# First feed-forward layer of a decoder block: the seven-product down stage with tokens standing, its sums turned once by VectorE

## The chip, the cores and the metric

The kernel runs on one core of a Trainium2 chip. The metric is the device time of one execution in microseconds (us), as the median of several. All matmuls work on float32 data that is split into a high and a low part.

## The reference

One decoder layer with 512 tokens (T) and 1024 channels (D): a half-step SwiGLU feed-forward layer, a token mixer, and a second half-step feed-forward layer, each with a norm before and one after. The change concerns only the first of them:

```
def swiglu(x, w_gu, w_down):
    gate, up = jnp.split(x @ w_gu, 2, axis=-1)
    return (jax.nn.silu(gate) * up) @ w_down

x = x + 0.5 * rms_norm(swiglu(rms_norm(x, ffn1_pre_g), ffn1_w_gu, ffn1_w_down), ffn1_post_g)
```

The hidden width is 2816, that is 22 chunks of 128.

## The kernel before

**Stages.** The hidden chunks of the first layer go in five groups: 0 to 3, 4 to 7, 8 to 11, 12 to 15 and 16 to 21. Group 0 is done plainly. For the others the gate and up products (`octo`) are made with seven products of blocks instead of eight, tokens standing in the array; the hidden values of four chunks are turned by VectorE's transposes (tile `za`), written to HBM (`h_a`) by four transfers on SyncE's queue, and read back (`hxa`) into the seven forms that the down stage needs (`seven_forms_of`). `Hidden.high` and `Hidden.low` make the high and the low part of each form.

**The down stage of a group** (`seven_down`) also takes seven products in place of eight, named a11, s3, a12, s2, s4, a22 and s1, for a block of weights of two chunks by 512 channels each. It is called for the groups that start at chunks 4, 8 and 12. The function `one` that it is given makes one product in two PSUM banks. Before, that is `by_channels`: 128 by 128 weights stand, 256 tokens move, three matmuls for each pair of a high and a low part, 24 matmuls a product. ScalarE copies the banks into a `stage` tile, and GpSimd adds the tile into HBM by a transfer with `accum_op=ALU.add`. The sums `yp_a` in HBM are laid out by channels, as the later steps want them: partitions are channels, columns are tokens. Group 0 writes them first.

**The last group** computes its down product plainly for eight chunks of 128 channels, c = 0 to 7. Before it, SyncE reads the sums back from HBM as `parts` (tiles `yp_a` in SBUF). The loop over c takes chunks 0 to 4 at once: six hidden chunks by three matmuls of 512 tokens into a bank `ya`, then VectorE adds the part (`Residual.chunk`, line 676 in the profile), ScalarE squares it, and GpSimd adds the square to `acca_r` (line 686). Chunks 5, 6 and 7 are late: `boundary` makes them in halves of 256 tokens (`ay`), first all three first halves, then the second halves. VectorE adds parts (L692) and squares (L705, L709), and in the middle of chunk 6's second half TensorE makes the sums of squares (`rms_r`, L550). While chunks are computed, ScalarE rounds later weights to their high part and VectorE subtracts to get the low part (`wlo_ad` for the down weights, `wlo_xl` for the mixer's, line 215).

In the same loop stand small tasks for the mixer that comes next: `load_gates`, `masks` (GpSimd fills and selects the attention mask in the tile `home`, VectorE copies it to `up`), `split_gates`, and `give_back`, by which GpSimd reads the residual's x back (`xT`).

**What sets the order.** Each engine executes its instructions in the order in which the program issues them, and so do the queues of transfers. `W` is the planner of weights: raw weights have five buffers (`tag="raw"`); when a raw buffer's last low part is made, it loads the next weights, or, where `W.owed` has an entry, calls that in its place. For the last group `W.owed` holds two entries that do nothing, so two loads are left out there:

```
            if f1 == FC:
                W.owed = [lambda: None] * 2
```

## Time and profile before

| | |
|---|---|
| time, median of 3 runs | 843.34 us (843.26 to 843.58) |
| the profiled execution's own time | 842.55 us |
| its span, from first to last instruction | 840.8 us |
| TensorE (PE) busy | 832.2 us, 99% |
| VectorE (DVE) busy | 723.8 us, 86% |
| ScalarE (ACT) busy | 520.9 us, 62% |
| GpSimd (POOL) busy | 162.6 us, 19% |
| the three down stages by channels, about | 155 to 175, 213 to 233, 271 to 292 us |
| the last group's down product and its late halves, about | 310 to 344 us |

In rows of the timeline the first two numbers are the start and the time taken, then come the engine, the line of the program, the operation, what it writes and reads, its shape and how many instructions the row holds; the brackets tell how long the engine was idle before it and what ended that. `SPq` and `POOLq` rows are issues of transfers. In rows of the windows, the columns are the window, its length, the busy time of each engine asked for (with its instructions), the granted TensorE clock, the share of the transfer engines and GB/s.

### The profile page before, as it was taken

Reading aid. Unit: us, or ns where it says so; the run is one execution under the profiler, and the core shown is the slowest. Engines: PE = TensorE matmul, PEld = TensorE weight load, DVE = VectorE, ACT = ScalarE, POOL = GpSimd, SP = SyncE. Lnnn points to the kernel's source line nnn. Section 1 sums busy time; section 2 is a strip of 40 time slices with the busy share of each in tenths; the row PEclk is TensorE's granted clock in tenths of the full one; section 3 lists DMA queues with packets and bytes.
Section 4 is the critical chain, followed back from the end, with each engine's and each line's share of the span. In section 5 each row is a group of like instructions: output and inputs, shape, how many; then the busy total and the mean of one; then the engine's idle time right before and its main releaser. Section 6 shows DMA issues by size and latency. Waiting matters only on the chain.

```text
span 840.8 us, 12378 instructions
## 1 busy us (share of the span) xinstructions
PE 832.2 (99%) x4504; PEld 718.9 (85%) x4504; DVE 723.8 (86%) x1026; ACT 520.9 (62%) x821; POOL 162.6 (19%) x178
## 2 busy tenths in 40 slices
PE   9999999999999999999999999999999999999996
PEld 8988888988988998987788899888888888888885
DVE  4978999998989965879889589799999899898996
ACT  6646756666666655556797456536758667666562
POOL 2023000140320333304531052002004114032001
PEclk9999999999999999999999999999999999999999
DMA  7249429398595799323511131169439939769842
GB/s 252 77 128 347 135 79 318 80 251 267 123 255 186 167 261 331 93 62 108 157 51 51 51 105 47 50 129 290 179 106 232 317 92 257 253 149 258 305 140 101
DMA packets 123614, 143.73 MB, mean 171 GB/s; under 512 B 23897, under 2 KB 81569, under 8 KB 123041
## 3 DMA queue, kind: packets, MB, share of 16 engines
q1 hardware_dynamic: 109232, 111.86, 42.0%
q0 software_dynamic: 14176, 30.94, 17.0%
q8 instruction: 35, 0.57, 0.3%
q14 instruction: 27, 0.21, 0.1%
q10 hardware_dynamic: 144, 0.13, 0.0%
HBM read 100.45 MB, written 40.89 MB: 168 GB/s over the span
## 4 chain that ended last, share of the span: by engine, by line
PE 96%; DVE 2%; DMA 1%; SPq 0%; issue 0%; ACT 0%; DVEq 0%; ACTq 0%
PE aa L951 10%; PE ab L951 10%; PE db L951 5%; PE da L951 5%; PE yaa L1347 3%; PE bb L951 3%; PE ba L951 3%; PE yda L1347 2%; PE ya L506 2%; PE ya L507 2%; PE ya L508 2%; PE aa L881 1%; PE a_first L1206 1%; PE yab L1884 1%; PE yab L1885 1%; PE yab L1886 1%
## 5 line engine op out<-in xcount | busy, mean ns | idle before, releaser
L1116 POOL DMA_DIRECT2D yp_a<-stage x42 | 36.8, 1064 | 182.6 <-ACT stage L1113 158.8
L1116 POOL DMA_DIRECT2D yp_b<-stage x42 | 36.4, 1084 | 144.3 <-ACT stage L1113 117.8
L506 PE MATMUL ya<-hha,whi_ad 128*128 128x512 f32 x62 | 24.1, 389 | 0.0
L507 PE MATMUL ya<-hla,whi_ad 128*128 128x512 f32 x62 | 24.1, 389 | 0.0
L508 PE MATMUL ya<-hha,wlo_ad 128*128 128x512 f32 x62 | 24.1, 389 | 0.0
L686 POOL TENSOR_TENSOR acca_r<-acca_r,sq_r 128x512 f32<-128x512 f32 x6 | 8.1, 1357 | 61.7 <-ACT sq_r L536 61.7
L1900 POOL DMA_DIRECT2D yp_b<-stage x8 | 4.3, 548 | 67.1 <-ACT stage L1899 67.1
L524 PE MATMUL an<-xh_mx,whi_xl 128*128 128x256 f32 x64 | 15.9, 289 | 0.0
L525 PE MATMUL an<-xh_mx,wlo_xl 128*128 128x256 f32 x64 | 15.5, 283 | 0.0
L2003 POOL TENSOR_TENSOR last<-yp,grow 128x512 f32<-128x512 f32 x3 | 3.9, 1290 | 57.2 <-DVE yp L1993 57.2
L2000 ACT ACTIVATE ysq<-yp 128x512 f32<-128x512 f32 (+1 forms) x8 | 4.8, 606 | 16.2 <-DVE yp L1993 16.2
L506 PE MATMUL gt<-xh_mx,whi_gt 128*128 128x512 f32 x32 | 14.3, 445 | 0.0
L508 PEld LDWEIGHTS ya<-hha,wlo_ad 128*128 128x128 f32 x62 | 11.6, 188 | 2.4
L506 PEld LDWEIGHTS ya<-hha,whi_ad 128*128 128x128 f32 x62 | 11.6, 188 | 2.4
L507 PEld LDWEIGHTS ya<-hla,whi_ad 128*128 128x128 f32 x62 | 11.6, 188 | 2.4
L536 ACT ACTIVATE sq_r<-yp_a 128x256 f32<-128x256 f32 (+1 forms) x10 | 5.0, 502 | 12.9 <-DVE yp_a L676 5.9
L506 PE MATMUL pq<-xh_mx,whi_q 128*128 128x512 f32 x32 | 12.8, 399 | 0.0
L506 PE MATMUL pub<-xh_f,whi_bu 128*128 128x512 f32 x32 | 12.6, 395 | 0.0
L508 PE MATMUL gt<-xh_mx,wlo_gt 128*128 128x512 f32 x32 | 12.6, 394 | 0.0
L506 PE MATMUL pgb<-xh_f,whi_bg 128*128 128x512 f32 x32 | 12.6, 393 | 0.0
L507 PE MATMUL gt<-xl_mx,whi_gt 128*128 128x512 f32 x32 | 12.6, 392 | 0.0
L508 PE MATMUL pgb<-xh_f,wlo_bg 128*128 128x512 f32 x32 | 12.5, 390 | 0.0
(2014 smaller groups left out, 3468.8 us busy)
## 6 DMA issues: line engine op xcount, KB each, us to landing
yp_a<-stage POOLq DMA_DIRECT2D x50, 256.0 KB, 9.1
yp_b<-stage POOLq DMA_DIRECT2D x50, 256.0 KB, 9.0
h_a<-za SPq DMA_DIRECT2D x16, 256.0 KB
hxa<-h_a SPq DMA_DIRECT2D x16, 256.0 KB
h_b<-zb SPq DMA_DIRECT2D x16, 256.0 KB
hxb<-h_b SPq DMA_DIRECT2D x16, 256.0 KB
xn<-in_x SPq DMA_DIRECT2D x8, 256.0 KB
xT_hbm<-xT POOLq DMA_DIRECT2D x2, 1024.0 KB, 9.8
```

Source lines behind the costliest of these rows:

```text
L506: pe.matmul(ps, hi[:, k, :], xh, start=start, stop=False)
L507: pe.matmul(ps, hi[:, k, :], xl, start=False, stop=False)
L508: pe.matmul(ps, lo[:, k, :], xh, start=False, stop=stop)
L524: pe.matmul(ps[:, sl], hi[:, k, :], xh, start=k == 0 and not goes_on, stop=False, skip_group_check=True)
L525: pe.matmul(ps[:, sl], lo[:, k, :], xh, start=False, stop=False, skip_group_check=True)
L881: pe.matmul(o, w[:, k, js], x, start=first and i + j + k == 0, stop=k == 3 and i == 2, skip_group_check=True)
L951: pe.matmul(b[tb], x[:, blk], w[:, k, :], start=first and q + k + j == 0, stop=q + k == 2 and j == 2, skip_group_check=True)
L1116: pool.dma_start(o, st.rearrange("p (a b) -> p a b", a=2) if len(o.shape) == 3 else st, accum_op=ALU.add)
L1206: pe.matmul(banks[j][:, HALF[0]], ws[j][part][:, k, :], n1.xs[k][xpart][:, HALF[0]], start=k == 0 and part == xpart, stop=stop and k == KD ...
L1347: pe.matmul(o, a[:, k, ms], x[:, js], start=first and i + k + m % 2 == 0, stop=k == 1 and i == 2, skip_group_check=True)
L1884: pe.matmul(banks[i], hh[:, js], hi[:, k, :], start=first and k == 0, stop=False, skip_group_check=True)
L1885: pe.matmul(banks[i], hh[:, js], lo[:, k, :], start=False, stop=False, skip_group_check=True)
```

## The change

The three seven-product down stages of the first layer use `by_dealt_tokens` instead of `by_channels`: 128 tokens stand, 512 channels move, 12 matmuls of 128x512 a product. The order of the hidden values in their forms is adapted (`by_blocks`, runs of 32 elements; the forms are fetched by two transfers of 512 KB instead of four of 256 KB). The sums are then laid out by tokens and gather in HBM in eight new tiles `yr_a`, 128 tokens by 512 channels each; the first product that touches a tile writes it, the others add.

They have to come back to channels once. `read_rows` reads four of these tiles, which hold one half of the channels, into a raw buffer (GpSimd's queue, in place of the empty entries of `W.owed`); `turn_sums` transposes them on VectorE and writes them to HBM (`yt_a`) by four transfers on SyncE's queue; `add_sums` adds 128 channels of that into a part in SBUF by a transfer on GpSimd's queue. The first half is turned right after the last group's gate and up stage and added before the loop over c; the second half is turned and added at c = 1. Group 0's own sums `yp_a` in HBM are now one tile for each c. `masks` moves from c = 0 to c = 2, and the decay factors (`decay_factor`, a score of small VectorE operations) from the first `octo` to the second.

VectorE before, from the low parts of the last hidden chunks (`hla`) to chunk 3's add; `wlo_ad_0_3352` is the low part of chunk 6's down weights, and the L676 rows are the adds of chunks 0, 1, 2 and 3:

```order
L891 TENSOR_TENSOR hla_3077<-g1a_3085,hha_3076 128x2x4x32
L1329 COPY up_590<-upf 128x512
L215 TENSOR_TENSOR wlo_ad_0_3284<-raw_ad__3210,whi_ad_0_3283 128x768
L215 TENSOR_TENSOR wlo_ad_1_3346<-raw_ad__3210,whi_ad_1_3345 128x768
L676 TENSOR_TENSOR yp_a_3322<-ya_3354,yp_a_3322 128x512
L676 TENSOR_TENSOR yp_a_3324<-ya_3355,yp_a_3324 128x512
L215 TENSOR_TENSOR wlo_ad_0_3352<-raw_ad__3281,whi_ad_0_3351 128x768
L676 TENSOR_TENSOR yp_a_3326<-ya_3409,yp_a_3326 128x512
```

The same place on VectorE after the change; `zy` are the turned sums, and chunk 6's low weights are now `wlo_ad_0_3124`:

```order
L898 TENSOR_TENSOR hla_2833<-g1a_2841,hha_2832 128x2x4x32
L1376 STREAM_TRANSPOSE zy_3086<-rows_a_2843 128x16x32 x4
L215 TENSOR_TENSOR wlo_ad_0_3050<-raw_ad__2976,whi_ad_0_3049 128x768
L215 TENSOR_TENSOR wlo_ad_1_3118<-raw_ad__2976,whi_ad_1_3117 128x768
L676 TENSOR_TENSOR yp_a_3097<-ya_3126,yp_a_3097 128x512
L1376 STREAM_TRANSPOSE zy_3172<-rows_a_2906 128x16x32 x4
L676 TENSOR_TENSOR yp_a_3099<-ya_3127,yp_a_3099 128x512
L1346 COPY up_590<-upf 128x512
L215 TENSOR_TENSOR wlo_ad_0_3124<-raw_ad__3047,whi_ad_0_3123 128x768
L676 TENSOR_TENSOR yp_a_3101<-ya_3201,yp_a_3101 128x512
```

The second half's transposes now stand between the adds of chunks 0 and 1, and the copy of the mask (`up`) has moved from ahead of both to right before chunk 6's low weights.

GpSimd before, from the last accumulates into HBM to the reads of x:

```order
L1116 DMA yp_a_594<-stage 128x512 x2
L1324 MEMSET home 128x8
L1326 MEMSET home 128x512
L1327 AFFINE_SELECT upf<-home 128x512
L1328 MEMSET home 128x512
L686 TENSOR_TENSOR acca_r_3320<-acca_r_3320,sq_r_3402 128x512
L686 TENSOR_TENSOR acca_r_3320<-acca_r_3320,sq_r_3429 128x512
L1317 TENSOR_TENSOR gates<-gates_raw,gates 128x512
L1357 DMA xT_3435<-xT_hbm_144 128x2048
```

GpSimd after, from the last add of the turned sums' first half (`yt_a_607`; three more such adds, and before them the eight reads of the row sums, stand ahead of it) to the split of the gates:

```order
L1381 DMA yp_a_3103<-yt_a_607 128x512
L1381 DMA yp_a_3105<-yt_a_608 128x512
L1381 DMA yp_a_3166<-yt_a_608 128x512
L1381 DMA yp_a_3168<-yt_a_608 128x512
L1381 DMA yp_a_3170<-yt_a_608 128x512
L686 TENSOR_TENSOR acca_r_3095<-acca_r_3095,sq_r_3187 128x512
L1341 MEMSET home 128x8
L1343 MEMSET home 128x512
L1344 AFFINE_SELECT upf<-home 128x512
L1345 MEMSET home 128x512
L686 TENSOR_TENSOR acca_r_3095<-acca_r_3095,sq_r_3221 128x512
L1334 TENSOR_TENSOR gates<-gates_raw,gates 128x512
```

The masks stood directly behind the accumulates; now all adds of the turned sums, of both halves, and the first square stand ahead of them. An add of the second half waits for `yt_a_608`, which is written from the transposes of `zy_3172`.

The diff, cut to its core:

```
     def high(self, name, x):
         hh = t2k(f"hh{name}", F32R)
-        act.copy(like(hh, x), x)
+        act.copy(*by_blocks(hh, x))
...
-    def by_channels(banks, w, h, first):
+    rows_hbm = {(tb, dh): hbm.tile([P, T], F32, name=f"yr_a{tb}{dh}") for tb in range(NB) for dh in range(2)}
+    turned_hbm = [hbm.tile([T, T], F32, name=f"yt_a{dh}") for dh in range(2)]
+    def by_dealt_tokens(banks, w, h, first):
         (hi, lo), (hh, hl_) = w, h
-        for m in range(4):
-            o, ms = banks[m // 2][:, HALF[m % 2]], slice(m * P, (m + 1) * P)
+        for i in range(2):
             for k in range(2):
-                js = HALF[k]
-                for i, (a, x) in enumerate(((hi, hh), (hi, hl_), (lo, hh))):
-                    pe.matmul(o, a[:, k, ms], x[:, js], ...)
+                blk = slice((2 * i + k) * P, (2 * i + k + 1) * P)
+                for j, (x, a) in enumerate(((hh, hi), (hh, lo), (hl_, hi))):
+                    pe.matmul(banks[i], x[:, blk], a[:, k, :], ...)
+    def read_rows(dh):
+        t = wpool.tile([P, NB * T], F32, tag="raw", name=f"rows_a{dh}", bufs=NRAW)
+        row_sums[dh] = [t[:, tb * T:(tb + 1) * T] for tb in range(NB)]
+        for tb in range(NB):
+            pool.dma_start(row_sums[dh][tb], rows_hbm[tb, dh])
+    def turn_sums(dh):
+        z = wide(f"zy{dh}")
+        for tb in range(NB):
+            dve.transpose(z.rearrange(...)[:, tb], row_sums[dh][tb].rearrange(...))
+        for i in range(4):
+            sync.dma_start(turned_hbm[dh][:, i * P:(i + 1) * P].rearrange("(j a) n -> a j n", a=32), ...)
+    def add_sums(c):
+        pool.dma_start(parts[c], turned_hbm[c // 4][(c % 4) * P:(c % 4 + 1) * P], accum_op=ALU.add)
...
-            h_hbm[f0] = hid.octo(f0, ... {2: [lambda: decay.append(decay_factor())]})
+            if g == 2:
+                beside[2] = [lambda: decay.append(decay_factor())]
-                seven_down(hid, before, by_channels, lambda half, dh, i: in_hbm[2 * dh + i][:, half], ...)
+                seven_down(hid, before, by_dealt_tokens, lambda half, dh, i: rows_hbm[2 * half + i, dh], ..., written=rows_written)
             if f1 == FC:
-                W.owed = [lambda: None] * 2
+                W.owed = [lambda: read_rows(0), lambda: read_rows(1)]
...
             xs = hid.last_chunks(f0, h_hbm[f0], {})
+            turn_sums(0)
...
+            for c in range(4):
+                add_sums(c)
         for c in range(KD):
-            if f1 == FC and c == 0:
+            if f1 == FC and c == 2:
                 neg = masks()
             if f1 == FC and c == 1:
                 ...
+                turn_sums(1)
+                for i in range(4, KD):
+                    add_sums(i)
```

More of the change, by code (lines that the diff above doesn't have):

```diff
@@ L795, in like, with by_blocks @@
     def like(t, x):
-        return t.rearrange("p (a b) -> p a b", a=2) if len(x.shape) == 3 else t
+        return t.rearrange("p (a b) -> p a b", a=x.shape[1]) if len(x.shape) == 3 else t
+    def by_blocks(t, x):
+        if len(x.shape) == 3 and x.shape[1] == 2 * NB:
+            return t.rearrange("p (b q n) -> p q b n", b=2, n=32), x.rearrange("p q (b n) -> p q b n", b=2)
+        return like(t, x), x
     class Hidden:
@@ L1017, in fetch @@
                 z = wide(f"hx{self.name}{f}")
+                if dealt_halves:
+                    for s in range(2):
+                        own = z[:, 2 * s * T:2 * (s + 1) * T]
+                        sync.dma_start(own.rearrange("p (j n) -> p j n", j=2), h_hbm[2 * s * P:2 * (s + 1) * P].rearrange("(j p) n -> p j n", p=P))
+                        x[s, 0], x[s, 1] = (own.rearrange("p (q s m) -> p s q m", s=2, m=64)[:, h] for h in range(2))
+                    return
                 for s in range(2):
@@ L1086, in last_chunks, with seven_down @@
             return [self.hs.pop(c) for c in range(f, f + 6)]
-    def seven_down(hid, f, one, part, forms, ahead, beside={}, keep=False):
+    def seven_down(hid, f, one, part, forms, ahead, beside={}, keep=False, written=None):
         free = [r_tile] + 3 * [acc_tile]
@@ L1115, in seven_down @@
                     o = part(half, dh, i)
[L1116 removed]
+                    if written is None or (half, dh, i) in written:
+                        pool.dma_start(o, st, accum_op=ALU.add)
+                    else:
+                        written.add((half, dh, i))
+                        pool.dma_start(o, st)
             for fn in beside.get(n, ()):
```

27 lines of the change are left out of this document (15 added, 12 removed).

## The prediction

> **What bounds the kernel now.** I read the first page's totals, then TensorE's busy time by stage, then the program order behind the changed stage, and last the rows that price each hop of that order.
>
> The page gives the span and each engine's share:
>
> ```profile
> span 840.8 us, 12378 instructions
> ...
> PE 832.2 (99%) x4504; PEld 718.9 (85%) x4504; DVE 723.8 (86%) x1026; ACT 520.9 (62%) x821; POOL 162.6 (19%) x178
> ```
>
> TensorE is busy for 99% of the span. So a shorter matmul stage is a gain, and any new hole in TensorE is a loss of its full length. The windows view gives TensorE's busy time (and its instructions) over two down stages by channels, of the first layer, and one by tokens, of the second layer. Each window is one stage of seven products:
>
> ```profile
> 154.76:174.90 20.14, 20.14 (x170) 1.00 0.64 150
> 271.37:291.52 20.15, 20.15 (x169) 1.00 0.63 141
> 621.78:640.84 19.06, 19.06 (x86) 1.00 0.53 125
> ```
>
> **What it removes.** Three down stages in the first layer go from 128x256 matmuls (some 170 each) to 128x512 ones (some 86). The second layer already has that shape: 20.15 - 19.06 = 1.09 us less a stage, three stages, -3.3 us. Both forms are 100% busy, so this term is on the path. Operations that only move their 32-element runs (hidden forms by blocks) keep their count and element counts; the 0.76 row for two 128x256 low parts below already has such runs, and I cost them at nothing. Ready forms fetched as two 512 KB transfers instead of four of 256 KB carry the same bytes, and the accumulating transfers into HBM stay as many, so these are nothing too. VectorE's decay operations move from the first seven-product group to the second:
>
> ```profile
> L1287 DVE SCALAR_TENSOR_TENSOR q<-q,s 128x4 f32<-128x4 f32 x6 | 1.0, 164 | 0.2
> ```
>
> About twenty of these at 0.164 us are 3.3 us of VectorE; TensorE is never idle there now, so I take 0 and leave 3 us to the upper end.
>
> **What it adds: a chain through HBM ahead of the last down products.** Before, the sums came back in the layout the residual adds need. Now VectorE must transpose them, SyncE write them, GpSimd add them into the parts, and only then can VectorE do the add. VectorE and GpSimd take instructions in order, so everything queued behind such a wait is late. What is queued there is the low half of chunk 6's weights, which TensorE needs. TensorE's two places in time before are the first matmul with those low weights, and the first matmul of the statistics, behind them:
>
> ```profile
> 334.50 0.28 PE L508 MATMUL ay<-hha,wlo_ad 128*128 128x256 f32 x1
> ...
> 341.82 0.50 PE L550 MATMUL rms_r<-mean_d,accb_r 128*128 128x1 f32 x4
> ```
>
> VectorE's timeline before, from the quad's last low parts to the last half-square of the statistics:
>
> ```profile
> 315.53 0.76 DVE L891 TENSOR_TENSOR hla<-g1a,hha 128x256 fp32r<-128x256 f32 x2 [0.47 <-ACT hha L888]
> 316.21 0.42 DVE L1329 CAST up<-upf 128x512 uint8<-128x512 f32 x1
> 316.55 1.82 DVE L215 TENSOR_TENSOR wlo_ad<-raw_ad__3210,whi_ad 128x768 fp32r<-128x768 f32 x2
> 319.39 1.37 DVE L676 TENSOR_TENSOR yp_a<-ya,yp_a 128x512 f32<-128x512 f32 x2 [1.02 <-PE ya L508]
> 320.68 0.95 DVE L215 TENSOR_TENSOR wlo_ad<-raw_ad__3281,whi_ad 128x768 fp32r<-128x768 f32 x1
> ...
> 328.83 1.22 DVE L215 TENSOR_TENSOR wlo_xl<-raw_xl__3349,whi_xl 128x1024 fp32r<-128x1024 f32 x1
> ...
> 336.30 0.41 DVE L692 TENSOR_TENSOR yp_a<-ay,yp_a 128x256 f32<-128x256 f32 x1
> ...
> 339.84 0.43 DVE L709 TENSOR_TENSOR accb_r<-accb_r,sq_r 128x256 f32<-128x256 f32 x1 [0.53 <-ACT sq_r L536]
> ```
>
> Chunk 6's low weights were done at 320.68 + 0.95 = 321.6, TensorE needed them at 334.50: a cushion of 12.9 us. GpSimd's timeline of the same stretch has the last accumulates, the masks and the first square:
>
> ```profile
> 298.48 4.41 POOL L1116 DMA_DIRECT2D yp_a<-stage  x5 [1.16 <-ACT p7a L903]
> 301.59 1.42 POOL L1324 MEMSET home<- 128x8 f32 x1
> 301.63 1.83 POOL L1326 MEMSET home<- 128x512 f32 x1
> 303.53 0.64 POOL L1327 TENSOR_SCALAR_AFFINE_SELECT upf<-home 128x512 f32<-128x512 f32 x1
> 304.23 0.53 POOL L1328 MEMSET home<- 128x512 f32 x1
> 322.85 1.30 POOL L686 TENSOR_TENSOR acca_r<-acca_r,sq_r 128x512 f32<-128x512 f32 x1 [18.10 <-ACT sq_r L536]
> ```
>
> Prices of the hops: the transposes of the first layer's forms have the new ones' size; the four writes of a turned form, and the reads that had to wait for their landing:
>
> ```profile
> 276.00 1.29 DVE L961 STREAM_TRANSPOSE za<-g1a 128x512 f32<-128x512 f32 x2
> ```
>
> ```profile
> 123.99 2.84 SPq L965 DMA_DIRECT2D h_a<-za  x4
> ```
>
> ```profile
> 130.17 1.40 SPq L1021 DMA_DIRECT2D hxa<-h_a  x3
> ```
>
> From the first write's issue to the released reads: 130.17 - 123.99 = 6.2 us. An accumulating transfer of 256 KB issued alone took 6.2 us to land (the DMA view of 296 to 298), a plain one 2.5 (65 to 66), and the tile's own view gives the spread, and GpSimd's time for one issue (minimum, median, maximum in ns):
>
> ```profile
> yp_a<-stage POOLq DMA_DIRECT2D x1, 256.0 KB, 6.2
> ```
>
> ```profile
> yp_a<-stage POOLq DMA_DIRECT2D x1, 256.0 KB, 2.5
> ```
>
> ```profile
> L1116 POOL DMA_DIRECT2D yp_a<-stage x42: 850/960/1834, 164.7 to 301.0; - x42
> ...
> DMA to landing us min/median/max: 2.5/9.1/14.0
> ```
>
> No row has an accumulate from HBM into SBUF; the 2.5 and the 9.1 bound it, and I take 6.5, next to the 6.2.
>
> The sum, in the clock of the trace before. VectorE is free at 316.3; the last accumulates are issued by 302.9, with the median latency of 9.1 they land by 312, and the reads of the row sums behind them have 4 us to come in: I take them as in.
> Transposes, 4 x 0.65 = 2.6: 318.9. Write, 6.2: 325.1. Accumulate, 6.5: 331.6. Chunk 0's add (0.69) and the second half's transposes (2.6): 334.9. Write, 6.2: 341.1. GpSimd stood waiting for that write; it now issues four accumulates (4 x 0.85 = 3.4): 344.5. The square queued behind them, 1.3: 345.8. The masks up to the select, which moved behind it (304.17 - 301.59 = 2.6): 348.4. VectorE's mask copy and chunk 6's low weights (0.42 + 0.95): 349.8. TensorE wanted them at 334.50: it waits 15.3 us.
>
> A second wait follows. VectorE still has a backlog ahead of the statistics: chunk 2 to 4's adds (3 x 0.69), chunk 7's low weights (0.95), three low parts of the mixer's weights (3 x 1.22), 6.7 us, to 356.5, and then the late adds and squares, 336.30 to 339.84 + 0.43, 4.0 us: 360.5. TensorE, 15.3 late, would be at the statistics at 341.82 + 15.3 = 357.1 and waits 3.4 more. Total delay 360.5 - 341.8 = 18.7; less 3.3: +15.4 us.
>
> The transfers of the residual's x (queued on GpSimd behind all this, issued some 7 us after the masks) end close to when the residual adds, themselves 18 us late, want them: I take 0. The row reads (2 MB) and the second pass over the sums share the queues with weights that are already loaded ahead: 0, with up to 3 us in the range.
>
> **Two rules weighed.** The clock: with TensorE idle after its last matmul, the windows view shows the granted clock fall (the last column but two), and the start shows twelve warm matmuls first slow and then fast:
>
> ```profile
> 838.00:839.00 1.00, 0.00 (x0) 0.00 (x0) 0.00 (x0) 0.00 (x0) 0.00 (x0) 0.71 0.84 291
> 839.00:840.80 1.80, 0.00 (x0) 0.00 (x0) 0.00 (x0) 0.00 (x0) 0.00 (x0) 0.50 0.02 5
> ```
>
> ```profile
> 1.43 2.93 PE L1193 MATMUL warm<-ident 128*128 128x128 f32 x12 [1.43 <-POOL ident masks.py:199]
> ...
> 5.97 1.60 PE L1193 MATMUL warm<-ident 128*128 128x128 f32 x12
> ```
>
> A 15 us hole would therefore restart cold; the same twelve cost 1.3 us more cold, so I price the restart at 1.5 to 2 us. It falls between the two waits and shortens the second (3.4 us): 0 in the sum, +2 at the upper end.
> The Trainium skill, "TensorE: Matmul & The Clock Gate", Part 1, says that the clock halves after an idle window of about 3.4 us and returns after as much sustained work. The rows above agree with the halving. By it the restart would lose about 1.7 us, and the sum would not change.
>
> The Trainium skill, "DMA: Bandwidth & Descriptors", section "Anatomy of one DMA — SWDGE (gpsimd) path", gives a transfer from GpSimd's queue 2 us plus its bytes at 436 GB/s, 2.6 us for 256 KB. The plain row's 2.5 agrees, the accumulating row's 6.2 does not. By that rule the one accumulate on the chain is 4 us shorter and the time some 4 us less; the measured 6.2 decides.
>
> **Rivals.** *The round trips are hidden.* TensorE gains 3.3 us and waits for nothing: 842.55 - 3.3 = 839.3 on the profiled clock, 840 on the median. For it: 12.9 us of cushion. Against it: two write-and-return trips, one behind the other, which alone are 12.4 us of writes and 6.5 us of accumulate from 318.9; even with a 2.5 us accumulate and writes of 4 the second write is in at 318.9 + 4 + 2.5 + 3.3 + 4 = 332.7, and GpSimd's 7 us come behind it. It decides only if the chain ends before 334.5, 15 us sooner than my sum. Chance 0.05, of which 0.01 is for a tie.
>
> *Short trips.* Accumulate at 2.5, writes 5.0 (issued faster than the 0.71 us each of the row): 4.0 + 2.4 = 6.4 us less, +9.0: 851.6 on the profiled clock, 852.3 on the median. For it: the plain 2.5. Against: the accumulating rows. Chance 0.25 for 849 to 855.
>
> *Congestion.* The accumulate takes the median's 9.1 (+2.6), the rows come 3 us later, the cold restart is not hidden (+2): +7.6, 866 on the median. For it: an accumulate of 14.0 exists. Against: the weights are mostly in. Chance 0.25 for over 862.
>
> **How the numbers follow.** The profiled execution took 842.55 us around a span of 840.8; the median of the runs is 843.34, 0.8 above it. Forecast: 842.55 + 15.4 = 857.95 on the profiled clock, 858.7 on the median; chance 0.45 for 855 to 862. The range reaches from the short trips to congestion, 851.5 to 866.5, which leaves out the hidden case and the tails of the other two. A measurement of this kernel can tell 0.2%, some 1.7 us. Faster has only the hidden case, 0.04; same 0.01; slower all others, 0.95.
>
> **What would show it.** Right: three down stages at 19.1 us; a hole in TensorE of about 15 us at a low-weight matmul of the late products, released by VectorE's low weights, and one of 2 to 5 us at the statistics; VectorE idle twice on a transfer, before chunk 0's add and not before chunk 2's; GpSimd's masks behind the second half's adds. Wrong: no hole ahead of the late products (the chain is shorter than the cushion), a hole elsewhere (the forms by blocks or the decay operations are late), or the down stages still at 20 us.

## The result, and the profile after

The changed kernel takes 869.73 us (median of 4 runs, 869.40 to 870.48), the kernel before 843.32 beside it. The ratio is 1.0314, with a 95% interval of 1.0296 to 1.0332. The forecast was 858.7 with a range of 851.5 to 866.5, so the direction was right and the size was not: +26.4 us instead of +15.4, 3.2 us above the top of the range. The profiled execution took 870.48 us around a span of 868.7.

The page's head, busy time (share of the span), and the granted clock in 40 slices of the span:

```profile
span 868.7 us, 11904 instructions
...
PE 835.0 (96%) x4252; PEld 709.2 (82%) x4252; DVE 730.7 (84%) x1034; ACT 519.5 (60%) x821; POOL 170.7 (20%) x194
...
PEclk9999999999999997799999999999999999999998
```

TensorE went from 99% to 96% busy, and two slices between 326 and 369 us ran below full clock. The waits of TensorE (total, times, longest) name two holes, the two that the forecast named:

```profile
PE ay L508 <- DVE wlo_ad L215: 20.3, 1, 20.3
PE rms_r L550 <- DVE accb_r L709: 3.9, 1, 3.9
```

TensorE's timeline gives their place. The first three rows are of after; the matmul at 352.53 in the fence behind them is of before, and is the same instruction as the one at 379.78, the mixer's first matmul that needs the second half's statistics:

```profile
353.96 0.58 PE L508 MATMUL ay<-hha,wlo_ad 128*128 128x256 f32 x1 [20.31 <-DVE wlo_ad L215]
...
367.48 0.61 PE L550 MATMUL rms_r<-mean_d,accb_r 128*128 128x1 f32 x4 [3.95 <-DVE accb_r L709]
...
379.78 0.47 PE L524 MATMUL an<-xh_mx,whi_xl 128*128 128x256 f32 x1
```

```profile
352.53 0.47 PE L524 MATMUL an<-xh_mx,whi_xl 128*128 128x256 f32 x1
```

So after stands behind before by 353.96 - 334.50 = 19.5 us at chunk 6's low weights, 367.48 - 341.82 = 25.7 at the statistics, 379.78 - 352.53 = 27.3 at that matmul of the mixer, and 868.7 - 840.8 = 27.9 at the end. Nearly all of the loss (27.3 of 27.9 us) arises between 333 and 380 us.

The gain is there too, in two of the three down stages. TensorE's windows, at the places of those shown of before:

```profile
154.00:174.00 20.00, 19.86 (x85) 1.00 0.36 90
213.00:232.00 19.00, 19.00 (x86) 1.00 0.58 140
```

The second does its 86 matmuls in 19 us; the first needs 20 for 85. From the first to the last matmul of a stage, before takes 20.32 us in each of the three, after 20.35, 19.20 and 19.20: two stages gain 1.12 us each, close to the forecast's 1.09, and the first gains nothing.

VectorE's timeline through the way back, then GpSimd's, then SyncE's queue (a part's read, `yp_a<-yp_a`, brings group 0's sums of a chunk into SBUF):

```profile
316.42 2.49 DVE L1376 STREAM_TRANSPOSE zy<-rows_a 128x512 f32<-128x512 f32 x4
...
332.76 0.69 DVE L676 TENSOR_TENSOR yp_a<-ya,yp_a 128x512 f32<-128x512 f32 x1 [12.15 <-DMA yp_a<-yt_a]
333.37 2.48 DVE L1376 STREAM_TRANSPOSE zy<-rows_a 128x512 f32<-128x512 f32 x4
...
352.22 0.83 DVE L1346 CAST up<-upf 128x512 uint8<-128x512 f32 x1 [15.79 <-POOL upf L1344]
352.97 0.94 DVE L215 TENSOR_TENSOR wlo_ad<-raw_ad__3047,whi_ad 128x768 fp32r<-128x768 f32 x1
...
356.66 2.22 DVE L215 TENSOR_TENSOR wlo_xl<-raw_xl__3121,whi_xl 128x1024 fp32r<-128x1024 f32 x1 [0.69 <-ACT whi_xl L210]
...
359.41 1.89 DVE L215 TENSOR_TENSOR wlo_xl<-raw_xl__3121,whi_xl 128x1024 fp32r<-128x1024 f32 x1
361.22 2.31 DVE L215 TENSOR_TENSOR wlo_xl<-raw_xl__3232,whi_xl 128x1024 fp32r<-128x1024 f32 x1
363.46 0.41 DVE L692 TENSOR_TENSOR yp_a<-ay,yp_a 128x256 f32<-128x256 f32 x1
```

```profile
327.08 1.81 POOL L1381 DMA_DIRECT2D yp_a<-yt_a  x2 [13.73 <-PE ya L507]
329.94 1.75 POOL L1381 DMA_DIRECT2D yp_a<-yt_a  x2 [1.04 <-DMA yp_a<-yp_a]
346.13 3.55 POOL L1381 DMA_DIRECT2D yp_a<-yt_a  x4 [14.44 <-DMA yt_a<-zy]
348.34 2.63 POOL L686 TENSOR_TENSOR acca_r<-acca_r,sq_r 128x512 f32<-128x512 f32 x1
...
351.55 0.63 POOL L1344 TENSOR_SCALAR_AFFINE_SELECT upf<-home 128x512 f32<-128x512 f32 x1
```

```profile
318.93 2.83 SPq L1378 DMA_DIRECT2D yt_a<-zy  x4
321.88 3.62 SPq L1418 DMA_DIRECT2D yp_a<-yp_a  x5
...
328.50 0.58 SPq L175 DMA_DIRECT2D raw_xl__3121<-in_w_in  x1
329.47 4.40 SPq L1429 DMA_DIRECT2D yp_a<-yp_a  x3
335.88 5.68 SPq L1378 DMA_DIRECT2D yt_a<-zy  x4
```

The releaser in the row at 327.08 is misnamed: by the landings in the trace the first write was in at 325.2 and the first part's read at 326.5, and GpSimd issued its add behind both.

Read together, this is the chain of the forecast, link by link: VectorE turns, SyncE writes, GpSimd adds, VectorE idles 12.15 us on that transfer before chunk 0's add; it turns the second half, SyncE writes again, GpSimd idles 14.44 us on that write, issues four adds, does the square and the masks; VectorE idles 15.79 us on the mask, copies it, and only then makes the low weights that TensorE wants. The all-engine windows (columns PE, PEld, DVE, ACT, POOL, then clock, transfer engines' share, GB/s) show what worked meanwhile:

```profile
335.00:345.00 10.00, 0.00 (x0) 0.00 (x0) 1.43 (x3) 1.96 (x4) 0.00 (x0) 0.65 1.05 300
345.00:350.00 5.00, 0.00 (x0) 0.00 (x0) 0.00 (x0) 0.00 (x0) 3.87 (x7) 0.50 1.03 253
354.00:358.00 4.00, 4.00 (x19) 4.00 (x20) 3.31 (x4) 3.46 (x5) 2.74 (x3) 0.50 0.35 92
```

From 335 to 345 the compute engines do almost nothing and the 16 transfer engines are full.

### The profile page after: what moved, and what is told of

It is laid out like the page before. It is cut to its first block, busy times and chain, and to the rows that moved or that the text cites. A ratio compares the mean times of both kernels' runs of the same rounds, so it can differ in the third digit from the quotient of the medians.

```text
span 868.7 us, 11904 instructions
## 1 busy us (share of the span) xinstructions
PE 835.0 (96%) x4252; PEld 709.2 (82%) x4252; DVE 730.7 (84%) x1034; ACT 519.5 (60%) x821; POOL 170.7 (20%) x194
## 4 chain that ended last, share of the span: by engine, by line
PE 82%; DVE 7%; DMA 3%; issue 3%; ACT 2%; POOL 1%; SPq 1%; DVEq 0%; ACTq 0%; POOLq 0%
PE ab L958 10%; PE aa L958 8%; PE db L958 5%; PE da L958 4%; PE bb L958 3%; PE ba L958 3%; DMA rows_a<-yr_a 1%; PE ya L506 1%; PE ya L507 1%; PE a_first L1223 1%; PE yaa L1363 1%; PE yab L1927 1%; PE yab L1929 1%; PE yab L1928 1%; PE ya L508 1%
## 5 line engine op out<-in xcount | busy, mean ns | idle before, releaser
L1130 POOL DMA_DIRECT2D yr_a<-stage x34 | 29.9, 1156 | 95.5 <-ACT stage L1126 75.4
L508 PE MATMUL ay<-hha,wlo_ad 128*128 128x256 f32 x36 | 11.7, 325 | 20.3 <-DVE wlo_ad L215 20.3
L508 PEld LDWEIGHTS ay<-hha,wlo_ad 128*128 128x128 f32 x36 | 8.4, 234 | 20.5 <-DVE wlo_ad L215 20.5
L1133 POOL DMA_DIRECT2D yr_a<-stage x8 | 4.3, 540 | 88.8 <-ACT stage L1126 88.8
L686 POOL TENSOR_TENSOR acca_r<-acca_r,sq_r 128x512 f32<-128x512 f32 x6 | 10.0, 1664 | 41.7 <-ACT sq_r L536 41.6
L676 DVE TENSOR_TENSOR yp_a<-ya,yp_a 128x512 f32<-128x512 f32 x5 | 3.4, 676 | 12.1 <-DMA yp_a<-yt_a 12.1
L1381 POOL DMA_DIRECT2D yp_a<-yt_a x8 | 7.1, 1180 | 29.2 <-DMA yt_a<-zy 14.4
```

The costliest lines, as they stand in the source:

```text
L508: pe.matmul(ps, lo[:, k, :], xh, start=False, stop=stop)
L686: eng.tensor_add(acc, acc, square(part, ALL, f"{self.name}{c}"))
L1130: pool.dma_start(o, st, accum_op=ALU.add)
```

## The experiments

The theory: the way back is a chain of transfers ahead of work that TensorE needs, and transfers set its length. The rivals: the order on VectorE and GpSimd (the masks and low weights queued behind the wait) makes the loss, and another order hides the chain; the price of the accumulation decides; something else in the change (the forms by blocks, the decay operations) loses time.

**No way back** (`no_return`). The sums of three groups stay in HBM and are missing from the output.

```
-                W.owed = [lambda: read_rows(0), lambda: read_rows(1)]
+                W.owed = [lambda: None] * 2
-            turn_sums(0)
-            for c in range(4):
-                add_sums(c)
-                turn_sums(1)
-                for i in range(4, KD):
-                    add_sums(i)
```

> The changed kernel without the way back: the sums by tokens gather in HBM, but are not read, turned or added, so the output lacks the seven-product sums of three groups. Theory (the chain through HBM makes the whole loss, the down stages gain, the moved decay operations cost 1.2 us in the first down stage): no hole in TensorE near 333, time 843.3 - 3.3 + 1.2 = 841.2 us. Rival (the form with tokens standing, or the layout of the forms, costs time by itself): 845 us or more.

Measured 841.28 us (840.67 to 842.03), ratio 0.9975 (0.9966 to 0.9984). Both holes are gone. So the way back costs 869.73 - 841.28 = 28.5 us, and the rest of the change is a small gain: what else it costs is less than what the faster stages bring.

**No way back, decay factors where they were** (`no_return_decay`).

```
-            if g == 2:
+            if g == 1:
```

(and the edit above.)

> As no_return, with the decay factors back in the first seven-product group. Theory: TensorE no longer waits for VectorE in the first down stage (gaps of 1.2 us between 165.9 and 167.8 in the changed kernel), 840.0 us, 1.2 us less than no_return. Rival (the gaps come from another cause): as no_return.

Measured 839.48 us (839.16 to 840.20), ratio 0.9954 (0.9942 to 0.9967): 1.8 us less than the run before it, with ranges that don't meet. TensorE's window over the first down stage now has 90 matmuls in its 20 us, against 85 above:

```profile
154.00:174.00 20.00, 20.00 (x90) 1.00 0.59 181
```

The move of the decay factors eats all of the first stage's gain: from its first to its last matmul that stage takes 19.20 us here and 20.35 in after. How it does so stands in the weight loads of after in that stage, where TensorE waits three times in a row:

```profile
166.35 0.19 PEld L1363 LDWEIGHTS yea<-whi_adt__1622,hhs 128*128 128x128 f32 x1 [0.46 <-ACT hhs L833]
166.84 0.19 PEld L1363 LDWEIGHTS yea<-wlo_adt__1623,hhs 128*128 128x128 f32 x1 [0.30 <-DVE wlo_adt__1623 L322]
167.44 0.19 PEld L1363 LDWEIGHTS yea<-whi_adt__1622,hls 128*128 128x128 f32 x1 [0.41 <-DVE hls L841]
```

These waits are 1.17 us. Where the other 0.6 of the 1.8 us lie is not shown.

**Decay factors alone** (`decay_back`): the same one-line edit, with the way back.

> The changed kernel with only the decay factors back in the first seven-product group. Theory (the chain starts at the landing of row sums and of late weights, which do not move with TensorE, so what TensorE gains ahead of the hole is lost in the hole): 869.2 to 869.9, no change beyond 0.5 us, a hole longer by 1.2 us. Rival (the gain counts): 868.5, 1.2 us less.

Measured 869.39 us (868.03 to 869.99), ratio 1.0312 (1.0296 to 1.0327). The 1.8 us that the move cost without the way back are 0.3 with it, and the ranges of the two kernels overlap, so that 0.3 can't be told from nothing. In its one profile the transposes begin 2.3 us sooner than in after (314.15), the statistics 1.6 sooner (365.91), the mixer's first matmul that needs them 0.8 sooner (378.96), and the end comes 0.4 sooner. So a gain ahead of the chain reached the end only in small part: of the 2.3 us, 0.7 were lost up to the statistics, 0.8 in a longer restart behind them (13.05 us against 12.3), and 0.4 later, which stays open.

**Masks out of the way** (`masks_early`). The mask is selected and copied in tiles of its own ahead of the turned sums, so that GpSimd and VectorE don't do it behind the second half's adds.

```
+            up_mask()
             turn_sums(0)
```

> The changed kernel with the mask's select and copy ahead of the sums' adds on GpSimd and VectorE, in scratch tiles of its own; all transfers as they were. Theory (instructions in order behind two round trips in series): chunk 6's low weights need only the first trip, so the hole of 20.3 us shrinks to about 4, but the second trip is then waited for at the statistics, by some 14 us: stats ready near 360 instead of 367, time about 863. Rival (the first hole is the whole loss): 850 to 853. Rival (queues of transfers set the end whatever the order): 868 or more.

Measured 867.70 us (866.10 to 867.81), ratio 1.0283 (1.0269 to 1.0297), not the 863 expected. TensorE's waits, and VectorE's row that now is late:

```profile
PE rms_r L550 <- DVE accb_r L709: 17.1, 1, 17.1
...
PE ay L508 <- DVE wlo_ad L215: 3.7, 1, 3.7
```

```profile
352.50 0.69 DVE L676 TENSOR_TENSOR yp_a<-ya,yp_a 128x512 f32<-128x512 f32 x1 [4.43 <-DMA yp_a<-yt_a]
```

The low weights are made at 335.86, as wanted, and the hole there falls from 20.3 to 3.7 us. But the second half's parts still come at 352.5, and the statistics want them: the wait moved there, 17.1 us. The order decides where TensorE waits, and only little of how long.

**Both halves turned at once** (`both_turned`), so that the second trip begins without waiting for the first.

```
             turn_sums(0)
+            turn_sums(1)
...
-                turn_sums(1)
```

> The changed kernel with the second half's transposes and writes right behind the first half's, ahead of the loop over chunks, so that the two writes overlap; adds where they were. Theory (two trips in series): the second write's landing moves from 345.6 to about 332, the first half's adds become some 5 us later since their parts are read behind the second write, chunk 6's low weights come at about 349 instead of 353.9, time 863 to 866. Rival (transfers saturate, the order of the trips is worth nothing): 869 or more. Rival (both trips in one, no queueing): 856 to 858.

Measured 870.92 us (869.03 to 871.79), ratio 1.0323 (1.0308 to 1.0337): the gain did not come, as the rival there said. GpSimd's row of its last three adds names what is late now:

```profile
345.55 2.66 POOL L1381 DMA_DIRECT2D yp_a<-yt_a  x3 [11.19 <-DMA yp_a<-yp_a]
```

No longer the turned write: the reads of group 0's parts, which stand behind it in the same transfers. These adds are issued at 345.55, only 0.6 us sooner than the second half's adds in after (346.13).

**Reads first** (`reads_first`): all eight reads of group 0's parts ahead of the turned writes, both halves at once, the eight adds in a row, masks early, decay back.

```
+            up_mask()
+            for c in range(KD):
+                parts[c] = t2k(f"yp_a{c}")
+                sync.dma_start(parts[c], in_hbm[c])
             turn_sums(0)
+            turn_sums(1)
...
-            for c in range(4):
+            for c in range(KD):
                 add_sums(c)
```

> The changed kernel with all of the chain's avoidable queueing taken away: the eight reads of group 0's sums stand ahead of the turned writes, both halves are turned and written together, the eight adds stand in one row, the mask's select and copy ahead of them, and the decay factors in the first seven-product group. Theory (a chain of transfers, made longer by what is queued ahead of them): the writes land near 324 and 329, the adds follow each other by about 2 us from 330 to 345; no or a short hole at chunk 6's low weights, 5 to 8 us at the statistics near 348, time 849 to 852. Rival (the accumulating transfers under load are the bound, whatever stands ahead): the last add near 353 as in both_turned, 858 or more.

Measured 865.01 us (861.78 to 866.50), ratio 1.0257 (1.0233 to 1.0281), not 849 to 852. The adds land in a row, but VectorE then waits for the mixer's weights, issued on SyncE's queue at 329.13 behind the writes and reads:

```profile
352.43 1.23 DVE L215 TENSOR_TENSOR wlo_xl<-raw_xl__3145,whi_xl 128x1024 fp32r<-128x1024 f32 x1 [13.18 <-ACT whi_xl L210]
```

In three orders three different things were late (the second write, the parts, the weights), each at 345 to 352 us. What the three have in common is the amount of transfers in front of the last of them. That this sets the time is a reading so far; the next two runs test it by leaving transfers out.

**Cheaper transfers** (`plain_adds`): the turned sums are copied into the parts, not added, and group 0's sums are not read at all (they are missing from the output).

```
-        pool.dma_start(parts[c], turned_hbm[...], accum_op=ALU.add)
+        pool.dma_start(parts[c], turned_hbm[...])
...
-                sync.dma_start(parts[c], in_hbm[c])
-                    sync.dma_start(parts[i], in_hbm[i])
```

> The changed kernel with the turned sums copied into the parts by plain transfers instead of added, and group 0's sums not read, so that the output lacks them: 2 MB less to read, and no accumulate. Theory (the hops' lengths are transfer time under load): the first copy lands near 328.5 instead of 332.7, the second write in 6.3 us instead of 9.8, near 338, chunk 6's low weights at 346 instead of 353.9, time 861 to 863. Rival (the hops are fixed latencies and issue times): within 1.5 us of the changed kernel, 868 to 870.

Measured 861.66 us (860.67 to 863.06), ratio 1.0224 (1.0208 to 1.0239): 8.1 us less with the order of the engines unchanged, the largest step of any run that kept a way back for all three groups, and inside the 861 to 863 that were expected.

**Copied over** (`copy_over`): only the first line of that edit, so that the reads of group 0's parts stay.

> The eight adds of the turned sums into the parts become plain copies over them (group 0's part is overwritten, so its sums are missing from the output); all reads of group 0's parts stay, unlike in the run that left out both. Theory A, the accumulation itself is the dear part (twice the transfer time per byte, which also slows the second write): most of the 8 us of that run come back, 861.5 to 864, and the second write lands in 6 to 7 us. Theory B, the reads of group 0's parts in front are the dear part: the first add still waits for a read that lands at 326.5, the second write still needs 9 to 10 us, and the time stays at 867 to 870. I lean to A, with about 2 us of the 8 left to the reads: 864.

Measured 867.13 us (864.47 to 868.79), ratio 1.0274 (1.0248 to 1.0300). I leaned to the accumulation. By the medians 2.6 of the 8.1 us go with it and 5.5 with the reads, the other way round. But the four runs spread over 4 us, and the profiled one (867.99) is among the longer, so the medians do not settle it. The profiles divide the chain itself. From the first transposes to chunk 6's low weights it takes 352.97 - 316.42 = 36.55 us in after, 347.70 - 315.56 = 32.14 in this kernel and 344.36 - 314.86 = 29.50 in `plain_adds`: of 7.05 us, 4.4 go with the accumulation and 2.65 with the reads. This kernel then loses part of its lead: it is 5.3 us ahead of after at the statistics (362.19 against 367.48) and 3.9 at the mixer's first matmul that needs them (375.90 against 379.78), a longer restart. So in the chain the accumulation is the larger part, and how the 8.1 us of the whole time divide stays open. GpSimd's rows show both:

```profile
325.87 0.55 POOL L1381 DMA_DIRECT2D yp_a<-yt_a  x1 [11.89 <-DMA yp_a<-yp_a]
...
342.26 2.16 POOL L1381 DMA_DIRECT2D yp_a<-yt_a  x4 [10.94 <-DMA yt_a<-zy]
```

The first copy still waits for a part's read, and the first trip, from the transposes to chunk 0's add, takes 16.1 us (16.3 in after, 13.9 without the reads). The second trip gets shorter: from the first write's issue to GpSimd's next issue 7.5 us against 346.13 - 335.88 = 10.25, and the four issues 2.16 against 3.55. What one accumulation costs the transfer engines is read from GpSimd's queue in the DMA view, packets, MB and share of 16 engines, of after (318 to 356) and of this kernel (318 to 349), each window holding just the eight transfers of 256 KB:

```profile
q0 software_dynamic: 1153, 2.10, 34.0%
```

```profile
q0 software_dynamic: 642, 2.10, 19.0%
```

That is 34.0% of 38 us, 12.9 us, against 19.0% of 31 us, 5.9 us: by the time of its packets, in the load of these stretches, an accumulation holds the engines 2.2 times as long as a copy.

**No squares** (`no_squares`): GpSimd's adds of the squares of chunks 1 to 4 are left out.

```
-                eng.tensor_add(acc, acc, square(part, ALL, ...))
+                if self.name != "r1":
+                    eng.tensor_add(acc, acc, square(part, ALL, ...))
```

> The changed kernel without the squares of chunks 1 to 4 (made by ScalarE, added by GpSimd), which are missing from the first norm. Theory (VectorE's low parts of the mixer's weights, 2.2, 1.9 and 2.3 us in the changed kernel against 1.22 before, are stretched by GpSimd's adds running beside them): the second and third at 1.2 to 1.3 us, the first still at 2 beside the split of the gates; time 1.5 to 2 us less, 868. Rival (they wait for their weights): as in the changed kernel, 869.7.

Measured 865.45 us (863.91 to 866.78), ratio 1.0270 (1.0252 to 1.0288): 4.3 us less, more than the 1.5 to 2 expected. ScalarE's squares that feed these adds go with them. The second hole is gone, the first is 19.5 us, and VectorE's mixer low parts take:

```profile
354.48 1.21 DVE L215 TENSOR_TENSOR wlo_xl<-raw_xl__3121,whi_xl 128x1024 fp32r<-128x1024 f32 x1
```

and 1.21 for the two others, against 2.22, 1.89 and 2.31 in after. GpSimd's tensor adds, which the delay had pushed beside them, stretched them by 6.4 - 3.6 = 2.8 us. ScalarE, whose squares are also gone, is not the cause: in after the third of them (361.22, 2.31 us) ran while ScalarE was idle, from 361.1 to 363.95. And in this kernel chunk 6's low part, 0.94 us in after, ran beside GpSimd's split of the gates (350.25, 1.43 us), with ScalarE idle, and took about twice as long:

```profile
350.48 2.00 DVE L215 TENSOR_TENSOR wlo_ad<-raw_ad__3047,whi_ad 128x768 fp32r<-128x768 f32 x1
```

The Trainium skill, "SBUF — State Buffer", section "Who interferes with whom", says that a VectorE instruction with both inputs in SBUF contends with a GpSimd instruction that reads SBUF; these rows agree. The 4.3 us hold more than the stretch: one square fewer stands ahead of the mask, and with the second hole the second cold restart is gone (11.0 us from the statistics to the mixer's first matmul that needs them, against 12.3 in after).

**Warm statistics** (`warm_stats`): 28 matmuls of the identity into an unused bank ahead of the statistics, to keep the clock up over the second hole.

```
+            if self.name == "r10":
+                for i in range(28):
+                    pe.matmul(ps[:, P:2 * P], ident, ident, start=True, stop=True)
```

> The changed kernel with 28 matmuls of 128x128 on the identity (3.7 us of work at full clock, results unused) put right ahead of the first statistics, where TensorE stands idle for 3.9 us. Theory (the second restart at half clock, 368 to 372 in the changed kernel, costs 1.6 us): the granted clock stays at 1.0 from 367 on, time 1.2 to 1.6 us less, 868.2. Rival (the restart is covered by VectorE's work): no difference, 869.7.

Measured 869.17 us (868.90 to 871.78), ratio 1.0318 (1.0304 to 1.0333), so no gain that can be told. TensorE's window behind the second hole, after first, then this kernel:

```profile
368.00:372.00 4.00, 4.00 (x20) 0.60 0.01 4
```

```profile
368.00:372.00 4.00, 4.00 (x36) 1.00 0.12 34
```

The clock did stay up, and the stretch from the statistics to the end was 1.4 us shorter than in after. But each of these matmuls ran as two, 6.4 us where I had counted 3.7, and the statistics began 2.8 us later (370.26). It shows the second cold restart and its size; it does not show that the restart can be had for less.

**Two groups by tokens, turned early** (`two_groups`). Only the first two down stages go by tokens, the third by channels. Their sums are read, turned and added by GpSimd into group 0's sums in HBM beside the last gate and up stage, so nothing stands ahead of the last down product. Masks and decay factors as before the change.

```
-            pool.dma_start(row_sums[dh][tb], rows_hbm[tb, dh])
+            pool.dma_start(held["rows_a"][:, tb * T:(tb + 1) * T], rows_hbm[tb, dh])
...
-            sync.dma_start(turned_hbm[dh][:, i * P:(i + 1) * P]..., z[...])
+            pool.dma_start(in_all[dh][:, i * P:(i + 1) * P]..., z[...], accum_op=ALU.add)
...
+                beside[4.5] = [lambda: (turn_sums(0), read_rows(1))] + beside.get(4.5, [])
+                beside[6] = beside.get(6, []) + [lambda: turn_sums(1)]
...
+                if g < 4:
                     seven_down(hid, before, by_dealt_tokens, ...)
+                else:
+                    seven_down(hid, before, by_channels, in_part, ...)
```

> Tokens standing only in the first two of the three down stages; the third goes by channels as before. The two stages' sums are read back during the last group's gate and up stage into raw buffers (whose weight loads move to later), transposed by VectorE in two halves there, and added into group 0's sums in HBM by GpSimd's accumulating transfers; from the last group's down product on everything stands as in the kernel before. Theory (the loss is only the chain's place right ahead of its use; 50 us earlier it is hidden): no hole in TensorE, two stages at 19.1 us and one at 20.15, 843.3 - 2.2 = 841.1 us. Rival (VectorE, 93% busy there, or the late weight loads set TensorE back): 844 us or more, gaps in TensorE between 270 and 300.

Measured 849.09 us (848.87 to 851.88), ratio 1.0081 (1.0067 to 1.0095): by far the best with a way back, and still slower than before. The two holes are gone, and small ones stand in their place: the largest of TensorE's waits, and GpSimd's row behind it:

```profile
PE aa L888 <- ACT ba L907: 2.6, 1, 2.6
```

```profile
286.84 7.32 POOL L1130 DMA_DIRECT2D yp_a<-stage  x6 [7.06 <-DMA yp_a<-zy]
```

GpSimd waited 7.06 us for its own turned sums to land before it could add the stage tiles of the running down stage into the same sums. That this is what holds TensorE there fits the rows, but was not tried by itself. The profile is of one of the two longer runs of the five (near 852 us), so this wait says little about the median.

**Two groups, in quarters** (`two_groups_b`): one raw buffer in place of two, the first channel half added in HBM as above, the second written plainly and added into parts 4 to 7.

```
+            if q < 2:
+                pool.dma_start(ov, zv, accum_op=ALU.add)
+            else:
+                pool.dma_start(ov, zv)
```

> As two_groups, with what held it up taken away: the rows are read and turned in four quarters of 256 channels through one raw buffer instead of two (so one weight load is put off, not two), the first half's quarters are added into HBM before the third down stage's own sums come, and the second half's quarters, turned inside that stage, are written by plain transfers and added into the parts of chunks 4 to 7 after the parts' reads. Theory (the chain costs nothing where it is not waited for): two_groups' gaps of 0.9, 0.9, 0.9 and 2.7 us between 280 and 302 are gone, 843 - 2.2 = 841 us. Rival (transfers and VectorE are too full for it anywhere in this stretch): 844 us or more, gaps after 316 at the adds of chunks 4 to 7 or at the mixer's weights.

Measured 861.35 us (860.00 to 862.46), ratio 1.0216 (1.0202 to 1.0230), not 841. The mixer's weights are late again, at 342.88 and once more at 351.90, and the statistics with them:

```profile
PE rms_r L550 <- DVE accb_r L709: 9.7, 1, 9.7
```

None of these versions with a way back beat the kernel before. One with all three stages by tokens whose way back cost nothing would take about the 839.5 us of `no_return_decay`, by my estimate.

## Why the prediction was right or wrong

The mechanism was right in its main links: the two holes, their releasers, the two idle times of VectorE (the first on a transfer, the second through GpSimd's mask, which stood behind the second trip), the masks behind the adds. The rival that the trips are hidden fell with the 20.3 us hole. What failed is the sizes, and with them two things that the sum left out: a wait for a part's read, and a second cold restart. The forecast on the profiled clock was 842.55 + 15.4 = 857.95, the profiled execution 870.48; the 12.5 us between them come from five terms, by the markers above.

**The chain to chunk 6's low weights: 353.9 instead of 349.8, +4.1.** The transposes ended at 318.9 as forecast, and by the landings in the trace the first write was in at 325.2 (forecast 325.1). Then "Accumulate, 6.5: 331.6" became 332.76: the transfer itself took 5.6 us from its issue at 327.08 to its landing, but it was issued some 1.9 us after the write landed, since it also waits for the read of group 0's part, a wait which the sum did not have (`copy_over` and `plain_adds` show it). That the term came out near is partly luck: the 6.2 behind it was called a transfer issued alone, but in that window, 296 to 298, GpSimd's queue alone held 103.8% of the transfer engines. "Write, 6.2: 341.1" is the term that failed most: the second write was issued at 335.88 and GpSimd went on at 346.13, 10.25 us later, instead of 6.2. By its landing at 345.6 it took 9.7 us; the first write had taken 6.3, by its landing too. The second met 16 engines at 1.03 to 1.05 of their time in the windows, with 1 MB of weights and three parts' reads issued just ahead, and SyncE's issue of its four transfers took 5.68 us instead of 2.83. The masks, 2.6 us in the sum, took 1.2 and gave part back.

Behind that lies a term that the forecast put at 0: the second pass over the sums, which shares the queues with weights taken to be "already loaded ahead". SyncE issues its transfers in program order, and the turned writes, which wait for VectorE's transposes, stand ahead of the parts' reads and of the mixer's weights. So these slid into the chain. SyncE's queue in before, the parts' first five reads and the mixer's first two loads:

```profile
304.92 6.02 SPq L1380 DMA_DIRECT2D yp_a<-yp_a  x5
...
315.72 0.51 SPq L175 DMA_DIRECT2D raw_xl__3349<-in_w_in  x1
...
319.32 0.55 SPq L175 DMA_DIRECT2D raw_xl__3440<-in_w_in  x1
```

In after the same three are issued at 321.88, 328.50 and 341.73. What the slide of the weights costs was not tried alone; the parts' reads as a whole cost 2.65 us of the chain (`plain_adds` against `copy_over`).

The Trainium skill, "DMA: Bandwidth & Descriptors", section "Anatomy of one DMA — SWDGE (gpsimd) path", gives a transfer from GpSimd's queue 2 us plus its bytes at 436 GB/s, 2.6 us for 256 KB. That is further off than the 6.5: the tile's own view of these eight gives 4.0, 7.1 and 9.1 us as minimum, median and maximum.

**The backlog of VectorE ahead of the statistics: 363.46 - 353.9 = 9.6 us instead of 6.7, +2.9.** The three mixer low parts were priced at 1.22 each. Before's own rows had the third of them at 1.74, beside a square of GpSimd (333.81, 1.48 us); the forecast's rows leave it out:

```profile
334.64 1.74 DVE L215 TENSOR_TENSOR wlo_xl<-raw_xl__3440,whi_xl 128x1024 fp32r<-128x1024 f32 x1 [0.50 <-ACT whi_xl L210]
```

In the new order GpSimd's gates and squares run beside all three: 6.4 us instead of 3.7. `no_squares` shows the cause. VectorE also waits 0.69 us for ScalarE's rounding of these weights.

**The second restart, +1.6.** The first one was hidden ahead of the second hole, as said (clock 0.50 from 354 to 358, TensorE then waits anyway). But the second hole, 3.95 us, let the clock fall again, and behind it nothing hides the restart: from the statistics to the mixer's first matmul that needs them it takes 379.78 - 367.48 = 12.3 us, against 352.53 - 341.82 = 10.7 before. The sum had no second restart.

**The gain, "less 3.3", did not reach the end, +3.3.** One stage of three gained nothing, since the move of the decay operations, taken as 0, cost 1.8 us (`no_return` against `no_return_decay`). Where the first hole begins, TensorE is at 353.96 - 20.31 = 333.65, only 0.85 us ahead of before, and the chain began no sooner: VectorE's transposes at 316.42, forecast from before's trace at 316.3. That start differs between the kernels' profiles (314.15 in `decay_back`, 314.86 in `plain_adds`), so part of the 3.3 may belong to this execution. In it ScalarE, ahead of it, waited for a transfer of weights, longer than before and until the same moment; its row of after, then of before:

```profile
312.60 0.84 ACT L210 CAST whi_ad<-raw_ad__2976 128x768 fp32r<-128x768 f32 x1 [5.95 <-DMA raw_ad__2976<-in_ffn_w_down]
```

```profile
312.39 0.84 ACT L210 CAST whi_ad<-raw_ad__3210 128x768 fp32r<-128x768 f32 x1 [3.91 <-DMA raw_ad__3210<-in_ffn_w_down]
```

The step that failed here is to subtract a gain of TensorE from a path that TensorE does not set. `decay_back` shows that such a gain, even where it moves the chain's start by 2.3 us, changes the time by no more than can be told (0.3).

**The rest, +0.6**, arises between 379.78 and the end, and stays open. The sum is 4.1 + 2.9 + 1.6 + 3.3 + 0.6 = 12.5. The median of the runs is 0.75 us below the profiled one.

The range failed because its congestion case changed one accumulate, the reads of the rows and one restart only (866). Against that case stood "the weights are mostly in", which the slide on SyncE's queue undid. The second write kept the same 6.2 in it, a price from a less loaded stretch: the windows have the transfer engines at 0.72 from 124 to 130.2 in before, and at 1.05 from 335 to 345 in after.

Shown by runs: that the way back is the whole loss (`no_return`); that moving what stands behind the wait moves the wait (`masks_early`, `both_turned`, `reads_first`); that fewer and cheaper transfers shorten the chain (`plain_adds`, `copy_over`); that GpSimd's tensor adds stretch VectorE's low parts (`no_squares`). Only read from the trace, and not tried alone: that the load of the mixer's weights ahead of the second write is part of its 10.25 us.

## What to carry to other kernels

Where a faster stage leaves its result in another layout, price the way back first, hop by hop, and price each hop in the load of its own stretch: four writes issued into full transfer engines took 10 us where four of the same size took 6 elsewhere. Look also at what slides: whatever stands behind a waiting instruction in an in-order queue moves into the same stretch. If three reorderings leave three different things late at the same moment, the amount of transfers is the first suspect; test it by leaving some of them out. Do not subtract a gain of one engine from a chain that another engine or a transfer sets, and look at which work a delay pushes side by side.

## What the hardware showed

- By the time of its packets, in these loaded stretches, an accumulating transfer of 256 KB held the 16 transfer engines 1.6 us (12.9 / 8), a plain one 0.74 (5.9 / 8). One issue took GpSimd 0.89 us (3.55 / 4) against 0.54 (2.16 / 4).
- VectorE's 128x1024 subtraction took 1.21 us with GpSimd's tensor adds left out (`no_squares`) and 1.9 to 2.3 beside them (after).
- The granted clock fell to 0.50 in a hole of 20 us, and behind a hole of 3.95 us it was 0.60 in the window from 368 to 372. The restart cost 1.6 us in the profile of after, 2.3 in that of `decay_back` (365.91 to 378.96) and 3.0 in that of `copy_over` (362.19 to 375.90), against 10.7 us for the same stretch before. The Trainium skill, "TensorE: Matmul & The Clock Gate", Part 1, says that the clock follows a free-running window of about 3.4 us, by which the price depends on where the window falls; the spread agrees, and so do the trace's records of the clock, in which the second spell at half clock lasts 3.4 us in after and 6.8 in `decay_back` and `copy_over`.
